# Loading the first B tile already cast, halving the B loads and reordering the right half in the head of a matmul + RMSNorm kernel on Trainium2

## The chip, the cores and the metric

The kernel runs on one core of one Trainium2 chip. The metric is the device time of one execution in microseconds (us). "Run time" below is that metric; "span" is the length of the traced part of an execution, about 1.8 us shorter. All positions ("at 39.46") are microseconds from the start of the span.

## The reference, cut to what matters

```python
m, k, n = 2048, 2048, 2048          # a, b, gamma are float32, eps = 1e-5
def reference(a, b, gamma, eps):
    x = np.matmul(a, b)
    rms = np.sqrt(np.mean(x ** 2, axis=-1, keepdims=True) + eps)
    return (gamma * x / rms).astype(np.float32)
```

## The kernel before

Sixteen blocks of 128 rows of A are multiplied by B. Most of the work (the later rows) uses seven products of quarter matrices instead of eight. The change touches only the **head**: the first four row blocks (rows 0 to 511), which are computed while B streams in for the first time.

- B comes in 16 tiles of 256 rows by 1024 columns: eight for the left half of its columns, eight for the right half. GpSimd issues these loads, which cast float32 to bf16 on the way (software-queue loads). Tile 0 of the left half is the exception: it is loaded as float32 on a hardware queue and cast by two engines.
- The **left half** has eight contraction steps. Step k needs the transposed A tile k and B tile k; within step k, PE also transposes A tile k+1. A step is 16 matmuls and 8 transposes.
- The **right half** has eight steps of 8 plain matmuls (row blocks 0 and 1) and three product matmuls (P2, P5 and P1 of row blocks 2 and 3; P1 lags one step).
- The **exit**: after the eighth right step come products 4, 3, 7 and 6. Meanwhile ScalarE and VectorE empty the banks, compute row norms of the next A block and scale it to 16 bits. PE transposes that block in the middle of product 7. I call this place the **turn**.

```python
# a0f: fp32 landing place of A tile 0; b0f: the same for B tile 0
nc.sync.dma_start(out=a0f, in_=a[0:HB * P, 0:W2].rearrange("(r p) k -> p r k", p=P))
for t in range(2):
    nc.scalar.dma_start(out=b0f[t], in_=b[t * P:(t + 1) * P, 0:HALF])

def load_b(j, kp):                       # one load for a whole B tile
    nc.gpsimd.dma_start(
        out=raw[j][kp],
        in_=b[kp * W2:(kp + 1) * W2, j * HALF:(j + 1) * HALF].rearrange("(t p) n -> p t n", p=P))

def load_head(kp):                       # A tile, then B tile
    nc.gpsimd.dma_start(out=ah(kp), in_=a[0:HB * P, kp * W2:(kp + 1) * W2].rearrange(...))
    load_b(0, kp)
# ... (cut: identities, 11 warm-up matmuls)

def transpose_first():
    # ... (cut: 8 fp32 transposes of A tile 0 into two banks)
    for t in range(2):
        cast_first = [lambda: nc.vector.tensor_copy(out=raw[0][0][:, t, :CH], in_=b0f[t][:, :CH]),
                      lambda: nc.scalar.copy(out=raw[0][0][:, t, CH:], in_=b0f[t][:, CH:])]
        move = [...]                     # (cut) VectorE moves the transposed A tile
        for work in (cast_first + move if t == 0 else move + cast_first):
            work()

# left half, per step kp (cut): load two to four tiles ahead, transpose_head(kp + 1) in its middle,
# 14 matmuls into 7 banks and 2 into a part bank

def stream_right(kp):
    order = [(g, kt) for kt in (2 * kp, 2 * kp + 1) for g in plain]
    if kp in (0, KP - 1):
        order.sort(key=lambda x: plain.index(x[0]))
    if kp == KP - 1:
        for m in (2, 5):
            pair_matmul(m, kp)
        pair_matmul(1, kp - 1)
    for g, kt in order:
        # ... plain matmul
    if kp < KP - 1:
        for m in (2, 5):
            pair_matmul(m, kp)
        if kp > 0:
            pair_matmul(1, kp - 1)
    else:
        pair_matmul(1, kp)

# exit
nc.scalar.copy(out=x22, in_=pair[2])
nc.vector.tensor_tensor(out=x22, in0=pair[5], in1=x22, op=ALU.add)
evict(plain, (2, 3))                     # banks 0, 1 by ScalarE; 2, 3 by VectorE
b_sums_in_place(1, KP - 1)
product(PAIR, 1, 4, pair[2], start=False)
row_norm(HB); row_norm(HB + 1)           # ScalarE
nc.vector.tensor_tensor(out=x22, in0=pair[1], in1=x22, op=ALU.subtract)
row_factor(HB)
product(PAIR, 1, 3, pair[5], start=False)
row_apply(HB)                            # VectorE: the 128x2048 scaling to fp16
# ... (cut)
product(PAIR, 1, 7, p7, within={5: [lambda: turn(HB, 0)]})
turn(HB, 1)
# ... (cut: product 6 and the whole body)
```

Of the kernel before, what the change touches and what calls it, by code (L numbers as in the profile page):

```python
# [17 lines left out]
def kernel(  # L18
# [13 lines left out]
    nc = tc.nc  # L32
# [32 lines left out]
    sums = [t_left, t_right]  # L65

    a0f = early[:, 0:2048].bitcast(FP32).rearrange("p (r k) -> p r k", r=HB)
    b0f = [early[:, 2048 + t * 2048:2048 + (t + 1) * 2048].bitcast(FP32) for t in range(2)]
    NAH = 6
    ah_slot = [early[:, 6144 + s * 1024:6144 + (s + 1) * 1024].rearrange("p (r k) -> p r k", r=HB)  # L70
               for s in range(NAH)]
# [16 lines left out]
        return (at_even, at_odd)[(mb // 2) % 2][:, mb % 2]  # L88


    nc.sync.dma_start(out=a0f, in_=a[0:HB * P, 0:W2].rearrange("(r p) k -> p r k", p=P))
    for t in range(2):
        nc.scalar.dma_start(out=b0f[t], in_=b[t * P:(t + 1) * P, 0:HALF])

    def ah(kp):
        return ah_slot[(kp - 1) % NAH]

    def load_b(j, kp):
        nc.gpsimd.dma_start(  # L99
            out=raw[j][kp],  # L100
            in_=b[kp * W2:(kp + 1) * W2, j * HALF:(j + 1) * HALF].rearrange(
                "(t p) n -> p t n", p=P))

    def load_head(kp):
        nc.gpsimd.dma_start(  # L105
            out=ah(kp),
            in_=a[0:HB * P, kp * W2:(kp + 1) * W2].rearrange("(r p) k -> p r k", p=P))
        load_b(0, kp)
# [16 lines left out]

        nc.gpsimd.tensor_copy(out=pace, in_=src)

    load_head(1)
    identity_f = t_left[:, 2, KP - 1, 0:2 * P].bitcast(FP32)
    make_identity(nc, identity_f)  # L130
    for kp in range(2, 4):
        load_head(kp)
    warm = sq_pool.tile([P, 2 * CH], BF16, name="sq")
# [7 lines left out]


    warm_bank = ps_a.tile([P, CH], FP32, name="acc")
    for _ in range(11):
        nc.tensor.matmul(warm_bank, warm[:, 0:P], warm[:, 0:CH], start=True, stop=True)

    gamma_sb = consts.tile([P, N], FP32, name="gamma_sb")
# [2 lines left out]
    def transpose_first():  # L150
        bank = [ps_t.tile([P, CH], FP32, name="tbank"), ps_a.tile([P, CH], FP32, name="acc")]
        view = [b.rearrange("p (r m) -> p r m", r=HB) for b in bank]
        for t in range(2):
            for r in range(HB):
                nc.tensor.matmul(view[t][:, r, :], a0f[:, r, t * P:(t + 1) * P], identity_f,
                                 is_transpose=True, start=(r == 0), stop=(r == HB - 1))
        for t in range(2):
            cast_first = [lambda: nc.vector.tensor_copy(out=raw[0][0][:, t, :CH],
                                                        in_=b0f[t][:, :CH]),
                          lambda: nc.scalar.copy(out=raw[0][0][:, t, CH:], in_=b0f[t][:, CH:])]  # L160
            move = [lambda h=h: nc.vector.tensor_copy(
                out=head_at[:, t, 2 * h:2 * h + 2, :], in_=view[t][:, 2 * h:2 * h + 2, :])
                for h in range(2)]
            for work in (cast_first + move if t == 0 else move + cast_first):
                work()

    def transpose_head(kp):
        bank = ps_t.tile([P, CH], FP32, name="tbank")
# [218 lines left out]
    def new_bank():  # L387
        return ps_a.tile([P, CH], FP32, name="acc")
# [74 lines left out]

    def stream_right(kp):

        order = [(g, kt) for kt in (2 * kp, 2 * kp + 1) for g in plain]
        if kp in (0, KP - 1):
            order.sort(key=lambda x: plain.index(x[0]))
        if kp == KP - 1:
            for m in (2, 5):  # L470
                pair_matmul(m, kp)
            pair_matmul(1, kp - 1)
        for g, kt in order:
            if kt == 0:
                banks[g] = new_bank()
            head_matmul(banks[g], *g, kt)
        if kp < KP - 1:
            for m in (2, 5):
                pair_matmul(m, kp)
            if kp > 0:  # L480
                pair_matmul(1, kp - 1)
        else:
            pair_matmul(1, kp)

    for kp in range(KP):
        load_later(1)
# [344 lines left out]
```

## Time and profile before

| | before |
|---|---|
| median run time | 222.89 us of three runs (222.73 to 223.05); with three more beside the changed kernel 222.63 us (222.40 to 223.05) |
| traced execution | run 222.97 us, span 221.2 us |
| first head matmul | 7.54 us |
| second left step starts | 12.30 us |
| sixth left step starts | 28.99 us |
| right half starts | 40.25 us |
| product 4 starts | 59.27 us |
| turn (transposes of the next A block) | 63.84 us |

The page's busy table, kernel before (engine, busy us, share of the span, instructions). PE is the bound.

```profile
PE 210.0 (95%) x1035; PEld 97.7 (44%) x1035; DVE 167.4 (76%) x330; ACT 128.1 (58%) x263; POOL 29.4 (13%) x59
```

The timeline of PE, kernel before. Each line is a group of like instructions: start, busy us, line, operation, output and inputs, count, and in brackets the idle time before it with what ended it.

```profile
7.54 2.88 PE L384 MATMUL acc<-b,head_at 128*128 128x512 bf16 x12
...
12.30 1.67 PE L384 MATMUL acc<-b,head_at 128*128 128x512 bf16 x7
...
16.19 1.67 PE L384 MATMUL acc<-b,head_at 128*128 128x512 bf16 x7
...
25.10 1.67 PE L384 MATMUL acc<-b,head_at 128*128 128x512 bf16 x7 [0.85 <-DMA b<-in_b_dram]
...
28.99 1.67 PE L384 MATMUL acc<-b,head_at 128*128 128x512 bf16 x7
...
40.25 1.89 PE L384 MATMUL acc<-b,head_at 128*128 128x512 bf16 x8
...
59.27 3.62 PE L289 MATMUL acc<-early,head_at 128*128 128x512 bf16 x16
...
63.84 0.62 PE L189 MATMUL tbank<-identity_h,head_at 128*128 128x128 f16 x8
```

A left step takes PE 3.90 us when nothing makes it wait (16.19 minus 12.30, 28.99 minus 25.10). The one long wait, 0.85 us, is for a B tile. The waits view of the weight loads (total us, times, longest):

```profile
PEld L189 <- DVE head_at L244: 0.4, 1, 0.4
```

The timeline of GpSimd, kernel before. It has eight loads in flight and holds the next one until an old one lands, so the ends of its idle times show when loads land.

```profile
12.54 0.70 POOL L99 DMA_DIRECT2D b<-in_b_dram  x1 [1.77 <-DMA b<-in_b_dram]
...
16.37 0.70 POOL L99 DMA_DIRECT2D b<-in_b_dram  x1 [1.78 <-DMA b<-in_b_dram]
```

A pair of A and B tiles lands every 3.83 us here (the next pairs take 4.06 and 4.91 us, then 3.82 again).

The windows view, kernel before. After the stretch and a granted clock come busy shares of PE, PEld, DVE, ACT and POOL with instruction counts, then PEclk, the mean busy share of the DMA engines, and GB/s moved.

```profile
5.00:6.00 1.00, 0.87 (x4) 0.10 (x2) 0.74 (x1) 0.62 (x1) 1.00 (x2) 1.00 1.12 337
6.00:7.00 1.00, 0.60 (x6) 0.63 (x7) 0.00 (x0) 0.00 (x0) 1.00 (x10) 1.00 0.78 196
```

At the start the queues still move float32 and reach 337 GB/s; once all loads cast, they settle near 200 GB/s written, twice that read.

### The profile page before, as it was taken

Reading aid. Unit: us, or ns where it says so; the run is one execution under the profiler, and the core shown is the slowest. Engines: PE = TensorE matmul, PEld = TensorE weight load, DVE = VectorE, ACT = ScalarE, POOL = GpSimd, SP = SyncE. Lnnn points to the kernel's source line nnn. Section 1 sums busy time; section 2 is a strip of 40 time slices with the busy share of each in tenths; the row PEclk is TensorE's granted clock in tenths of the full one; section 3 lists DMA queues with packets and bytes.
Section 4 is the critical chain, followed back from the end, with each engine's and each line's share of the span. In section 5 each row is a group of like instructions: output and inputs, shape, how many; then the busy total and the mean of one; then the engine's idle time right before and its main releaser. Section 6 shows DMA issues by size and latency. Waiting matters only on the chain.

```text
span 221.2 us, 3022 instructions
## 1 busy us (share of the span) xinstructions
PE 210.0 (95%) x1035; PEld 97.7 (44%) x1035; DVE 167.4 (76%) x330; ACT 128.1 (58%) x263; POOL 29.4 (13%) x59
## 2 busy tenths in 40 slices
PE   7899899999999999999999999999999999999950
PEld 2445454444455444444444444444444444444430
DVE  2428789999988898969696639855794759797691
ACT  3110001830698898678945997389738995334570
POOL 7634323220000001200110002000200000000040
PEclk9999999999999999999999999999999999999996
DMA  6999999999938596956799249955798349044045
GB/s 184 223 202 209 203 208 210 211 211 238 426 114 357 187 291 120 316 230 150 219 308 397 79 88 266 367 221 95 187 302 367 69 90 381 32 190 193 1 190 191
DMA packets 36321, 47.13 MB, mean 213 GB/s; under 512 B 21969, under 2 KB 26065, under 8 KB 34897
## 3 DMA queue, kind: packets, MB, share of 16 engines
q0 software_dynamic: 9936, 23.33, 41.7%
q1 hardware_dynamic: 25936, 22.29, 33.6%
q10 hardware_dynamic: 432, 1.31, 2.0%
q8 instruction: 8, 0.13, 0.2%
q14 instruction: 9, 0.07, 0.1%
HBM read 34.60 MB, written 16.78 MB: 232 GB/s over the span
## 4 chain that ended last, share of the span: by engine, by line
PE 83%; DMA 8%; POOL 3%; DVE 2%; issue 1%; ACT 1%; DVEq 0%; ACTq 0%; POOLq 0%
PE acc L289 69%; PE acc L384 12%; DMA b<-in_b_dram 8%; POOL early L105 1%; POOL b L99 1%; DVE x L709 1%; PE tbank L415 1%; PE tbank L172 1%; DVE x L712 1%; ACT sq L307 0%; PE tbank L189 0%; PE acc L189 0%; DVE a L709 0%; ACT sq L778 0%; DVE x L786 0%
## 5 line engine op out<-in xcount | busy, mean ns | idle before, releaser
L289 PE MATMUL acc<-b,s 128*128 128x512 bf16 x408 | 92.1, 379 | 0.0
L289 PEld LDWEIGHTS <-s 128*128 128x128 f16 (+1 forms) x512 | 49.9, 98 | 59.9 <-DVE s L264 0.4
L384 PE MATMUL acc<-b,head_at 128*128 128x512 bf16 x176 | 41.9, 379 | 1.0 <-DMA b<-in_b_dram 0.9
L307 ACT ACTIVATE sq<-x 128x512 bf16<-128x512 f32 x54 | 34.0, 630 | 6.9 <-DVE x L709 3.0
L366 DVE SCALAR_TENSOR_TENSOR x<-x,r,gamma_sb 128x1024 f32<-128x1024 f32 x28 | 34.8, 1281 | 0.7
L223 ACT ACTIVATE sq<-a 128x1024 bf16<-128x1024 f32 x24 | 25.3, 1054 | 2.4 <-DMA a<-in_a_dram 1.9
L384 PEld LDWEIGHTS <-head_at 128*128 128x128 bf16 x176 | 16.8, 98 | 20.6 <-issue 1.9
L246 ACT ACTIVATE head_at<-a,s 128x2048 f16<-128x2048 f32 x10 | 20.0, 1998 | 3.7 <-DVE s L233 3.7
L426 ACT COPY x<-acc 128x512 f32<-128x512 f32 x6 | 3.4, 586 | 25.7 <-PE acc L384 25.7
L289 PEld LDWEIGHTS <-head_at 128*128 128x128 f16 (+1 forms) x112 | 10.9, 98 | 13.2
L289 PE MATMUL acc<-early,head_at 128*128 128x512 bf16 x64 | 14.5, 379 | 0.0
L289 PEld LDWEIGHTS <-at_even 128*128 128x128 f16 x96 | 9.4, 98 | 11.3
L289 PE MATMUL acc<-early,s 128*128 128x512 bf16 x56 | 14.4, 379 | 0.0
L264 DVE TENSOR_TENSOR s<-head_at 128x1024 f16<-128x1024 f16 (+5 forms) x22 | 13.4, 635 | 0.1
L596 DVE TENSOR_TENSOR x<-x,x 128x512 f32<-128x512 f32 x9 | 6.2, 692 | 8.8 <-ACT x L594 8.3
L99 POOL DMA_DIRECT2D b<-in_b_dram x15 | 10.6, 706 | 16.0 <-DMA b<-in_b_dram 13.4
L578 ACT COPY x<-acc 128x512 f32<-128x512 f32 x9 | 5.2, 574 | 11.6 <-PE acc L289 11.5
L289 PE MATMUL acc<-t_left,s 128*128 128x512 bf16 x48 | 11.3, 379 | 0.0
L280 DVE TENSOR_TENSOR b<-b 128x1024 bf16<-128x1024 bf16 x16 | 10.8, 684 | 0.2
L289 PE MATMUL acc<-t_left,head_at 128*128 128x512 bf16 x48 | 10.9, 379 | 0.0
L289 PE MATMUL acc<-t_left,at_even 128*128 128x512 bf16 x48 | 10.8, 379 | 0.0
L289 PE MATMUL acc<-early,at_even 128*128 128x512 bf16 x48 | 10.8, 379 | 0.0
(111 smaller groups left out, 216.7 us busy)
## 6 DMA issues: line engine op xcount, KB each, us to landing
out_dram<-x SPq DMA_DIRECT2D x30, 512.0 KB, 3.8
a<-in_a_dram POOLq DMA_DIRECT2D x10, 1024.0 KB, 8.7
b<-in_b_dram POOLq DMA_DIRECT2D x15, 512.0 KB, 17.5
a<-in_a_dram POOLq DMA_DIRECT2D x4, 512.0 KB, 16.6
early<-in_a_dram POOLq DMA_DIRECT2D x7, 256.0 KB, 14.8
early<-in_b_dram ACTq DMA_DIRECT2D x2, 512.0 KB, 5.9
gamma_sb<-in_gamma_dram POOLq DMA_DIRECT2D x1, 1024.0 KB, 14.8
early<-in_a_dram SPq DMA_DIRECT2D x1, 512.0 KB, 5.5
```

The source lines that it names most:

```text
L99: nc.gpsimd.dma_start(out=raw[j][kp], in_=b[kp * W2:(kp + 1) * W2, j * HALF:(j + 1) * HALF].rearrange("(t p) n -> p t n", p=P))
L223: nc.scalar.activation(out=junk, in_=a32[mb][:, h * HALF:(h + 1) * HALF], func=ACTF.Square, scale=2.0 ** -8, accum_out=n2[:, h:h + 1])
L246: nc.scalar.activation(out=a16[mb], in_=a32.pop(mb), func=ACTF.Copy, scale=factor.pop(mb))
L264: nc.vector.tensor_tensor(out=sum_of(g, s)[:, lo:hi, :], in0=x[:, lo:hi, :], in1=y[:, lo:hi, :], op=op)
L280: nc.vector.tensor_tensor(out=flat[:, 1:3, :], in0=flat[:, 1:3, :], in1=flat[:, 0::3, :], op=ALU.add)
L289: nc.tensor.matmul(bank, lhsT[:, kp, :], rhs, start=(start and kp == 0), stop=(kp == KP - 1), skip_group_check=not start)
L307: nc.scalar.activation(out=sq[:, 0:CH], in_=src, func=ACTF.Square, scale=inv_sqrt_n, accum_out=msq[mb][:, c:c + 1])
L366: nc.vector.scalar_tensor_tensor(out=x, in0=x, scalar=inverse_of[mb], in1=gamma_sb[:, h * HALF:(h + 1) * HALF], op0=ALU.mult, op1=ALU.mult)
L384: nc.tensor.matmul(bank, head_at[:, kt, r, :], head_rhs(c, kt), start=(kt == 0), stop=(kt == KT - 1))
L426: copy(out=x_chunk(*g), in_=banks[g])
L578: nc.scalar.copy(out=c, in_=one[1])
L596: nc.vector.tensor_tensor(out=t, in0=t, in1=x12, op=ALU.add)
```

## The change

The intent: start the head sooner and let PE begin on half a B tile. B tile 0 comes by the same casting loads as the others, so its landing place and four casts go. A tile 0 comes by halves on the two hardware queues. Every B tile comes in two half loads of 128 rows. In the right half each step uses the first half tile, then P2 (which needs only that half), then the second half, then P5. Warm-up matmuls go from eleven to eight.

```diff
-    nc.sync.dma_start(out=a0f, in_=a[0:HB * P, 0:W2].rearrange("(r p) k -> p r k", p=P))
-    for t in range(2):
-        nc.scalar.dma_start(out=b0f[t], in_=b[t * P:(t + 1) * P, 0:HALF])
+    for h, queue in enumerate((nc.sync, nc.scalar)):
+        queue.dma_start(out=a0f[:, 2 * h:2 * h + 2, :],
+                        in_=a[2 * h * P:(2 * h + 2) * P, 0:W2].rearrange("(r p) k -> p r k", p=P))
 
     def load_b(j, kp):
-        nc.gpsimd.dma_start(
-            out=raw[j][kp],
-            in_=b[kp * W2:(kp + 1) * W2, j * HALF:(j + 1) * HALF].rearrange(
-                "(t p) n -> p t n", p=P))
+        for t in range(2):
+            lo = kp * W2 + t * P
+            nc.gpsimd.dma_start(out=raw[j][kp][:, t, :],
+                                in_=b[lo:lo + P, j * HALF:(j + 1) * HALF])
 
-    load_head(1)
+    load_b(0, 0)
     identity_f = t_left[:, 2, KP - 1, 0:2 * P].bitcast(FP32)
     make_identity(nc, identity_f)
+    load_head(1)
 
-    for _ in range(11):
+    for _ in range(8):
         nc.tensor.matmul(warm_bank, warm[:, 0:P], warm[:, 0:CH], start=True, stop=True)
 
     # (cut) in transpose_first the four casts go; VectorE and ScalarE each move one transposed bank
 
     def stream_right(kp):
-        # (cut) the order of before, shown above
+        def plain_matmuls(order):
+            for g, kt in order:
+                if kt == 0:
+                    banks[g] = new_bank()
+                head_matmul(banks[g], *g, kt)
+
+        first, second = ([(g, 2 * kp + t) for g in plain] for t in range(2))
+        if kp == 0:
+            plain_matmuls(x for both in zip(first, second) for x in both)
+            pair_matmul(2, kp)
+            pair_matmul(5, kp)
+            return
         if kp == KP - 1:
             pair_matmul(1, kp - 1)
+        plain_matmuls(first)
+        pair_matmul(2, kp)
+        plain_matmuls(second)
+        pair_matmul(5, kp)
+        pair_matmul(1, kp if kp == KP - 1 else kp - 1)
```

More of the change, by code (lines that the diff above doesn't have):

```diff
@@ L67 @@
     a0f = early[:, 0:2048].bitcast(FP32).rearrange("p (r k) -> p r k", r=HB)
-    b0f = [early[:, 2048 + t * 2048:2048 + (t + 1) * 2048].bitcast(FP32) for t in range(2)]
     NAH = 6
@@ L156, in transpose_first @@
                                  is_transpose=True, start=(r == 0), stop=(r == HB - 1))
-        for t in range(2):
-            cast_first = [lambda: nc.vector.tensor_copy(out=raw[0][0][:, t, :CH],
-                                                        in_=b0f[t][:, :CH]),
-                          lambda: nc.scalar.copy(out=raw[0][0][:, t, CH:], in_=b0f[t][:, CH:])]
-            move = [lambda h=h: nc.vector.tensor_copy(
-                out=head_at[:, t, 2 * h:2 * h + 2, :], in_=view[t][:, 2 * h:2 * h + 2, :])
-                for h in range(2)]
-            for work in (cast_first + move if t == 0 else move + cast_first):
-                work()
+        for t, copy in enumerate((nc.vector.tensor_copy, nc.scalar.copy)):
+            for h in range(2):
+                copy(out=head_at[:, t, 2 * h:2 * h + 2, :], in_=view[t][:, 2 * h:2 * h + 2, :])
     def transpose_head(kp):
@@ L464, in stream_right @@
     def stream_right(kp):
-        order = [(g, kt) for kt in (2 * kp, 2 * kp + 1) for g in plain]
-        if kp in (0, KP - 1):
-            order.sort(key=lambda x: plain.index(x[0]))
+        def plain_matmuls(order):
[9 more added lines that the diff above has]
+            return
         if kp == KP - 1:
-            for m in (2, 5):
-                pair_matmul(m, kp)
             pair_matmul(1, kp - 1)
-        for g, kt in order:
-            if kt == 0:
-                banks[g] = new_bank()
-            head_matmul(banks[g], *g, kt)
-        if kp < KP - 1:
-            for m in (2, 5):
-                pair_matmul(m, kp)
-            if kp > 0:
-                pair_matmul(1, kp - 1)
-        else:
-            pair_matmul(1, kp)
+        plain_matmuls(first)
[3 more added lines that the diff above has]
+        pair_matmul(1, kp if kp == KP - 1 else kp - 1)
     for kp in range(KP):
```

## The prediction

> **What bounds the kernel now.** PE. The busy table gives it 210.0 of 221.2 us; the chain of waits is PE alone from 25.10 to 208.16 us. What can move is the head, 0 to 59 us. The timeline shows PE starting a left contraction step at 12.30, 16.19, 20.18, 25.10, 28.99, 32.89 us: 3.90 us each (16 matmuls and 8 transposes), but for one of 4.9 us, in which PE waited 0.85 us for B. GpSimd's idle periods end as B tiles land: 12.54, 16.37, 20.43, 25.34, 29.16 us, so 3.82 us a step. The windows view shows about 207 GB/s written there, all casting. In the right half PE takes 2.37 us a step and DMA 2.48. Before 12.30 PE idles 1.46 us at the start, 0.53 for A0, and about 1 us more.
>
> **What the change does.**
> 1. B0 arrives cast: four casts go (0.62+0.74, 0.62+0.43 us on ACT and DVE); the second pair began only at 8.70 us, when the fp32 B0 landed. A0's transposed tiles are moved by DVE and ACT. The source bytes stay. I estimate DMA work until B1 has landed from the rates seen (about 420 GB/s for fp32, 207 written for casts): 7.6 us before, 7.6 after. So no bandwidth is won; order is.
> 2. A0 no longer competes with fp32 B0 on the other hardware queue. All queues share the DMA engines, as the Trainium skill says (DMA: Bandwidth & Descriptors, "Issuing engines are not separate DMA queues"); here A0 landed at 6.4 us, after B0's first half at 5.2. I expect A0 near 5.0, first head matmul near 6.3 (was 7.54), B1's step near 10.8 (was 12.30).
> 3. Half loads: PE may start a step one half (about 1.25 us) before the whole tile has landed. The second half is needed about 1.9 us into the step. That slack swallows the 0.85 us wait.
> 4. The right half needs the last tile's second half for only 6 matmuls (1.3 us), before for nearly 12.
> 5. Eight warm-ups end near 4.9 us. The trace shows the faster weight loads from 5.27. The Trainium skill (TensorE: Matmul & The Clock Gate, Part 1) puts the release after about 3.4 us of activity, so eight barely suffice.
>
> **How much survives.** PE could be 2.3 us early at the fifth step. Then: the first right step takes both halves of its tile at once (cost about 0.4 us); DVE has no idle time from 37.0 to 61.7 us and PE already waits 0.4 us on the scaled A rows at 63.8 us, so another 0.4 us may go there. The rest, PE-bound, moves along. Net estimate: 1.5 us.
>
> **Prediction: 221.4 us, 220.4 to 222.7 (8 in 10). Faster by over 2%: 0.01; within 2%: 0.97; slower: 0.02.**
>
> **What would show it.** Right: first head matmul before 6.6 us, second contraction step before 11.2 us, no wait over 0.5 us on B at the fifth step, product 4 starting near 57.6 us (was 59.27). Wrong: B0's first half landing after 7 us (step 2), B waits in each step (3), long PE waits near 60 us (survival), matmuls 0.43 us apart after 6 us (5).
>
> **What would make it wrong.** Sixteen more software DMAs lower the rate; GpSimd has only eight loads in flight (it held its ninth until the first landed), now 4 MB of source, before 6; the software B0 starts late; a cold PE costs up to 1.5 us. Upward: the 4.9 us step was chance.

## The result, and the profile after

| | before | after |
|---|---|---|
| median run time, six runs each | 222.63 us (222.40 to 223.05) | 222.84 us (222.60 to 222.93) |
| ratio after / before | | 1.0006 (95%: 0.9993 to 1.0019) |
| traced execution: run, span | 222.97, 221.2 us | 222.79, 221.0 us |

Ratios here and below are the mean time of one kernel's fast runs over that of the other's in the same rounds, so they are not quite the ratio of the medians quoted beside them. The time did not move.

The busy table of the page, kernel after: the same PE time, slightly less VectorE and ScalarE work (the casts are gone), more GpSimd (the additional loads).

```profile
PE 210.2 (95%) x1032; PEld 98.1 (44%) x1032; DVE 165.5 (75%) x326; ACT 127.2 (58%) x263; POOL 35.7 (16%) x76
```

The timeline of PE, kernel after, at the same places.

```profile
6.55 3.20 PE L378 MATMUL acc<-b,head_at 128*128 128x512 bf16 x12
...
11.68 1.67 PE L378 MATMUL acc<-b,head_at 128*128 128x512 bf16 x7
13.69 0.62 PE L166 MATMUL tbank<-identity,early 128*128 128x128 bf16 x8 [0.34 <-DMA early<-in_a_dram]
...
23.89 1.67 PE L378 MATMUL acc<-b,head_at 128*128 128x512 bf16 x7
...
28.20 1.67 PE L378 MATMUL acc<-b,head_at 128*128 128x512 bf16 x7
...
39.46 1.89 PE L378 MATMUL acc<-b,head_at 128*128 128x512 bf16 x8
...
58.45 3.62 PE L283 MATMUL acc<-early,head_at 128*128 128x512 bf16 x16
...
63.55 0.62 PE L183 MATMUL tbank<-identity_h,head_at 128*128 128x128 f16 x8 [0.40 <-DVE head_at L238]
```

Against this one trace of before, PE is 0.99 us ahead at its first head matmul, 0.62 at the second left step, 0.79 at the sixth, 0.79 at the right half and 0.82 at product 4. At the turn the lead is 0.29 us, because a 0.40 us wait has appeared. Two things are to be explained: why a start about a microsecond sooner and the removal of a 0.85 us wait do not add up in the left half, and why half a microsecond is lost between 58 and 64 us.

The waits view of the weight loads: first the line for the A tiles in the kernel before, then in the kernel after (total us, times, longest).

```profile
PEld L172 <- DMA early<-in_a_dram: 0.2, 1, 0.2
```

```profile
PEld L166 <- DMA early<-in_a_dram: 3.1, 7, 0.8
```

In the kernel after, the weight loads of the transposes wait for their A tile in all seven left steps. The wait for B became a wait for A. PE itself loses time at two of them: 0.50 us in the second step (at 13.69) and 0.40 us in the fifth (at 25.80; the view puts that wait down to VectorE's L269, which ended 0.04 us after the A tile had landed; in e1, e3 and e5 it names the A tile). Together that is the 0.92 us, within rounding, by which the sixth step is later than four steps of 3.90 us after the second.

The windows view, kernel after, same stretches as before.

```profile
5.00:6.00 1.00, 1.00 (x7) 1.00 (x6) 0.06 (x1) 0.00 (x0) 1.00 (x2) 1.00 1.00 92
6.00:7.00 1.00, 1.00 (x6) 0.63 (x5) 0.70 (x2) 0.20 (x1) 1.00 (x3) 1.00 0.84 84
```

For two microseconds the casting loads move 92 and 84 GB/s, less than half of the 203 GB/s that the same view shows between 8 and 9 us. The busy share of the DMA engines is 1.00 and 0.84 there, 1.39 between 8 and 9 us.

The chain of waits between 57 and 69 us, first before, then after (start, us, what).

```profile
57.49 1.73 PE acc L384 x8
59.22 4.75 PE acc L289 x22
63.97 0.49 PE tbank L189 x8
```

```profile
58.18 0.23 PE acc L283
...
58.50 0.69 DVE x L507
...
59.71 0.68 DVE x L420
60.39 0.60 DVE b L274
60.99 0.60 DVE x L513
...
62.21 1.29 DVE head_at L238
...
63.55 0.62 PE tbank L183 x8
```

Before, the chain stays on PE. After, it leaves PE at the exit and goes through VectorE's bank work and scaling until the turn.

What heads that chain shows in the timelines of ScalarE and VectorE. The first fence is of before, the second of after. The first line of each is ScalarE's copy of P2's bank, the second VectorE's addition of P5 to it.

```profile
57.10 0.59 ACT L511 COPY x<-acc 128x512 f32<-128x512 f32 x1 [10.60 <-PE acc L289]
...
58.68 0.68 DVE L512 TENSOR_TENSOR x<-acc,x 128x512 f32<-128x512 f32 x1
```

```profile
57.35 0.59 ACT L506 COPY x<-acc 128x512 f32<-128x512 f32 x1 [11.64 <-PE acc L283]
...
58.50 0.69 DVE L507 TENSOR_TENSOR x<-acc,x 128x512 f32<-128x512 f32 x1 [0.47 <-ACT x L420]
```

PE is 0.82 us ahead, yet the copy starts 0.25 us *later*. In the old eighth step P2 and P5 were finished before the plain matmuls; now P2 ends after half of them and P5 after all. VectorE is only 0.18 us ahead.

### The profile page after: what moved, and what is told of

Read it like the earlier page. It is cut to its first block, busy times and chain, and to the rows that moved or that the text cites. A ratio compares the mean times of both kernels' runs of the same rounds, so it can differ in the third digit from the quotient of the medians.

```text
span 221.0 us, 3043 instructions
## 1 busy us (share of the span) xinstructions
PE 210.2 (95%) x1032; PEld 98.1 (44%) x1032; DVE 165.5 (75%) x326; ACT 127.2 (58%) x263; POOL 35.7 (16%) x76
## 4 chain that ended last, share of the span: by engine, by line
PE 80%; DMA 9%; DVE 5%; POOL 2%; issue 1%; ACT 1%; DVEq 0%; ACTq 0%; POOLq 0%
PE acc L283 67%; PE acc L378 11%; DMA early<-in_a_dram 4%; DMA b<-in_b_dram 4%; POOL b L100 1%; DVE x L704 1%; PE tbank L409 1%; PE tbank L166 1%; POOL early L104 1%; DVE head_at L238 1%; DVE x L707 1%; DVE t_left L269 0%; PE tbank L183 0%; ACT sq L301 0%; PE acc L183 0%
## 5 line engine op out<-in xcount | busy, mean ns | idle before, releaser
L283 PE MATMUL acc<-b,s 128*128 128x512 bf16 x408 | 93.2, 379 | 0.0
L378 PE MATMUL acc<-b,head_at 128*128 128x512 bf16 x176 | 43.3, 381 | 0.0
L100 POOL DMA_DIRECT2D b<-in_b_dram x32 | 17.2, 539 | 20.3 <-DMA b<-in_b_dram 14.4
L283 PEld LDWEIGHTS <-head_at 128*128 128x128 f16 (+1 forms) x112 | 10.9, 98 | 13.2
L125 POOL COPY pace<-x 128x1 f32<-128x1 f32 x4 | 1.7, 413 | 66.3 <-DVE x L600 65.1
L274 DVE TENSOR_TENSOR b<-b 128x1024 bf16<-128x1024 bf16 x16 | 10.8, 683 | 0.2
L283 PE MATMUL acc<-t_left,head_at 128*128 128x512 bf16 x48 | 10.9, 379 | 0.0
L283 PE MATMUL acc<-t_left,at_even 128*128 128x512 bf16 x48 | 10.8, 379 | 0.0
```

The costliest lines, as they stand in the source:

```text
L100: nc.gpsimd.dma_start(out=raw[j][kp][:, t, :], in_=b[lo:lo + P, j * HALF:(j + 1) * HALF])
L274: nc.vector.tensor_tensor(out=flat[:, 1:3, :], in0=flat[:, 1:3, :], in1=flat[:, 0::3, :], op=ALU.add)
L283: nc.tensor.matmul(bank, lhsT[:, kp, :], rhs, start=(start and kp == 0), stop=(kp == KP - 1), skip_group_check=not start)
L378: nc.tensor.matmul(bank, head_at[:, kt, r, :], head_rhs(c, kt), start=(kt == 0), stop=(kt == KT - 1))
```

## The experiments

"Before" in each table is the kernel before, run on the same chip. No difference below reaches 1%, so the milestones of the traces, one trace per kernel, carry most of the argument. Two theories of the left half stood against each other.

- **Supply.** The left half ends when its bytes have come. A and B are the same bytes in both kernels, so a lead at the start is spent on waiting for tiles.
- **Head.** The lead is only smaller than it should be, because the first software loads are slow; a faster start would carry through.

For the exit: **order** (the new eighth step delays the banks) against **chance** or a cost of the earlier arrival itself.

### e8_before_again: is the trace of before typical?

No edit.

> The kernel before, unchanged, for a second trace: its profiled run was 0.3 us above the median of its later runs. If the 0.85 us wait for B at the fifth step (25.1 us) is its regular behaviour, it is here again with 0.5 to 1.1 us; if it was chance, it is below 0.3 us and the kernel before reaches product 4 at about 58.4 us instead of 59.27, with nothing left to gain from slack there.

| | before | e8 |
|---|---|---|
| median | 222.49 us (222.29 to 223.00) | 222.45 us (222.34, 222.57) |
| ratio | | 0.9997 (0.998 to 1.0014) |

The wait for B at the fifth step was there again (0.6 us), so it is regular in being there, not in its length. And the first trace was of a late run: this one starts its sixth left step at 28.58 (28.99 there), product 4 at 58.83 (59.27 there) and the turn at 63.40 (63.84 there). Most of that lateness lies in the long step itself: 0.08 us at the second step, 0.16 at the fourth, 0.41 at the fifth, and no more than 0.44 from there on. Against it the changed kernel leads by 0.38 us at product 4 and is 0.15 us *behind* at the turn. That, and not the 0.29 us against the first trace, agrees with the medians.

### e1_right_old: the right half in its old order

```diff
 def stream_right(kp):          # body of the kernel before; half loads and the new head stay
-        first, second = (...)
+        order = [(g, kt) for kt in (2 * kp, 2 * kp + 1) for g in plain]   # ... as before
```

> The change without its right-half order: matmuls of the right half as before, half loads and the new head kept. Exit theory (the change loses its lead at the end of the right half, because products 2 and 5 and the four plain banks now finish later relative to product 4, so ScalarE and VectorE start the copies, the row norms and the scaled A rows later): product 4 starts near 58.5 us as in the changed kernel, perhaps up to 0.3 later because the last tile's second half is needed at once, but VectorE no longer idles 0.47 us at 58 us, PE waits under 0.15 us on the scaled A rows (0.40 in the changed kernel), and the time is 0.3 to 0.6 us below the changed kernel, 0.3 to 0.8 below the kernel before. Rival (the row norms are late for a reason outside the right half's order, by DMA or ScalarE): the PE wait stays near 0.4 us and the time stays within 0.15 us of the changed kernel.

| | before | e1 |
|---|---|---|
| median | 222.56 us (222.36 to 223.02) | 223.05 us (222.28 to 224.15) |
| ratio | | 1.0025 (1.0002 to 1.0049) |

The wait at the turn is gone (turn at 63.42). But the time became longer and scattered by nearly 2 us. The trace, that of the 224.15 us run, shows new PE waits of 0.73 us at 77.23 and 0.46 us at 83.05. The source is a load that GpSimd issues near 64 us, told under e3.

### e3_exit_old: only the eighth right step in its old order

```diff
         if kp == KP - 1:
+            for m in (2, 5):
+                pair_matmul(m, kp)
             pair_matmul(1, kp - 1)
+            plain_matmuls(x for both in zip(first, second) for x in both)
+            pair_matmul(1, kp)
+            return
         plain_matmuls(first)
         pair_matmul(2, kp)
         plain_matmuls(second)
         pair_matmul(5, kp)
-        pair_matmul(1, kp if kp == KP - 1 else kp - 1)
+        pair_matmul(1, kp - 1)
```

> The change with only the last step of the right half (the eighth) in its order of before: products 2 and 5 first, then product 1 of the step before, then the plain products bank by bank. Exit theory: as in the run with the whole old right order, the PE wait on the scaled A rows goes under 0.15 us, and the time is 0.3 to 0.5 us below the changed kernel, against at most 0.3 us of new PE waiting for the last tile's second half. Rival: PE waits near 0.4 us all the same and the time is within 0.15 us of the changed kernel.

| | before | e3 |
|---|---|---|
| median | 222.56 us | 223.77 us (222.82 to 224.85) |
| ratio | | 1.0053 (1.0031 to 1.0075) |

Again the turn's wait went (turn at 63.28) and again the time rose. Two lines of this trace, of GpSimd and of VectorE, then the line of GpSimd in the kernel after:

```profile
64.14 1.57 POOL L119 DMA_DIRECT2D a<-in_a_dram  x1 [10.78 <-ACT x L522]
...
64.31 1.28 DVE L238 TENSOR_SCALAR head_at<-a,s 128x2048 f16<-128x2048 f32 x1
```

```profile
64.40 0.53 POOL L119 DMA_DIRECT2D a<-in_a_dram  x1 [11.32 <-DVE s L226]
```

Issuing the load took 1.57 us where it takes 0.53 elsewhere, and it ended 0.12 us after VectorE's 128x2048 scaling (64.31 + 1.28 = 65.59; 64.14 + 1.57 = 65.71). The Trainium skill, page "SBUF — State Buffer", sections "SBUF: two separate sides" and "A bandwidth-pool intuition that's wrong (but worth ruling out)", warns of this as the "DVE blocks DMA" trap: a load issued by GpSimd needs descriptors, GpSimd cannot write them while VectorE holds the port that they share, and the wait lasts until "DVE-end + ~115 ns". This trace agrees within its rounding. In the traces without the trouble in which GpSimd issues this load, it began at least 0.25 us ahead of VectorE (e10; 0.35 us or more in all others), here and in e1 only 0.17 us. The A block came late: ScalarE began its norms at 71.62 us, in the kernel after at 70.13, in e1 at 71.90. PE then waited 0.60 us at 76.95 and 0.46 us at 82.77.

### e5_sync_loads: that block by a hardware queue

On top of e3 (`load_block` is given the queue as an argument; cut):

```diff
-    load_block(HB + 2)
-    load_block(HB + 3)
+    load_block(HB + 2, nc.sync)
+    load_block(HB + 3, nc.sync)
```

> The run with the eighth right step in its old order lost its PE wait at 63 us but ended 1 us later, with 1.57 us (0.53 in the changed kernel) for GpSimd's issue of the next A block and a PE wait of 0.6 us near 77 us. Here the same kernel issues that block and the one after it from the SyncE hardware queue. Port theory (GpSimd's descriptor writing is locked out by VectorE's 1.28 us scaling of an A block, which starts 0.17 us after the issue, so the block lands about 1.5 us late): the PE waits near 77 and 82.5 us go, the row norms of that block start before 70.5 us (71.6 there), the time falls to about 222.0 us, 0.2 to 0.5% under the kernel before, and the scatter (222.8 to 224.9 there) shrinks to under 0.6 us. Rival (the block is late because the queue or HBM is slow at that time): ScalarE still starts on the block after 71.2 us and the time stays above 223.

| | before | e5 |
|---|---|---|
| median | 222.49 us (222.29 to 223.00) | 222.55 us (222.38 to 222.96) |
| ratio | | 1.0003 (0.9991 to 1.0015) |

The waits near 77 and 83 us are gone and the scatter is down from 2.0 to 0.6 us. The lock is thus the reason for e3's longer time, and for e1's, where the same issue took 1.57 us, too. The hoped-for gain over before did not come: product 4 starts at 58.77 us. In this trace the right half began late, at 39.76 us, and took 19.01 us, as in the kernel before (19.02). In e1 and e3 it began at 39.60 and 39.38 us but took 19.25 and 19.33; the likely reason is that the old order needs the last half tile of B at once (e3's waits show 0.17 us for it, e1's none). All three reach product 4 between 58.71 and 58.85 us, hardly sooner than e8 (58.83).

### e7_old_head: the old head, the rest of the change

The kernel before with half loads and the new right order; A tile 0, B tile 0 and the warm-ups as before.

```diff
 def load_b(j, kp):
-        nc.gpsimd.dma_start(out=raw[j][kp], in_=...)
+        for t in range(2):
+            lo = kp * W2 + t * P
+            nc.gpsimd.dma_start(out=raw[j][kp][:, t, :], in_=b[lo:lo + P, j * HALF:(j + 1) * HALF])
 def stream_right(kp):
-    ...    # order of before
+    ...    # order of after
```

> Half loads and the new right-half order with the head of before (B0 in fp32 on the ScalarE queue, A0 in one piece, 11 warm-ups). If the new head gives the lead of about 0.6 us at the second step that the two traces show, this kernel starts the second step at 12.0 to 12.4 us; its A tiles then land just in time, the right half starts about 0.2 to 0.6 us later than in the changed kernel, and it is 0.1 to 0.5 us slower than it. If the head's lead is lost to the A tiles anyway, both reach the right half within 0.15 us of each other, and the times agree within 0.15 us.

| | before | e7 |
|---|---|---|
| median | 222.49 us (222.29 to 223.00) | 223.01 us (222.91 to 223.13) |
| ratio | | 1.0022 (1.0009 to 1.0035) |

This is the cleanest evidence of the exit's cost. First fence: e7. Second: the kernel before of e8.

```profile
58.82 3.62 PE L289 MATMUL acc<-early,head_at 128*128 128x512 bf16 x16
...
63.92 0.62 PE L189 MATMUL tbank<-identity_h,head_at 128*128 128x128 f16 x8 [0.40 <-DVE head_at L244]
```

```profile
58.83 3.62 PE L289 MATMUL acc<-early,head_at 128*128 128x512 bf16 x16
...
63.40 0.62 PE L189 MATMUL tbank<-identity_h,head_at 128*128 128x128 f16 x8
```

Product 4 starts at the same time, the turn 0.52 us later, and the medians differ by 0.52 to 0.56 us. The order costs this without any lead, so it is no cost of arriving early. Nor is it the half loads, in which e7 also differs from e8: e1, e3 and e5 have them with the old order and no wait at the turn. The half loads gained nothing with the old head: the sixth left step starts at 28.57, and at 28.58 in e8. Against the kernel after, e7 differs in the head alone. The kernel after is 0.60 us ahead of it at the second step and 0.37 us at the sixth, at the right half and at product 4 (58.45 against 58.82), as the first branch of the expectation had it. By time it is 0.17 us ahead, by medians. So part of the head's lead does come through.

### e2_turn_late: give the turn the time that it lacks

```diff
-    product(PAIR, 1, 7, p7, within={5: [lambda: turn(HB, 0)]})
+    product(PAIR, 1, 7, p7)
+    turn(HB, 0)
     turn(HB, 1)
```

> The change with the first transposes of the scaled A rows after product 7 instead of inside it (0.65 us later). If the 0.40 us PE wait on these rows is what ate the lead, PE has no wait there over 0.15 us and the time falls by 0.2 to 0.45 us below the changed kernel, unless the later transposes create a new wait of PE in front of the next group's first product, which the wait view would show at VectorE's sums near 68 to 71 us. If the lead had been lost for another reason, no change within 0.1 us.

| | before | e2 |
|---|---|---|
| median | 222.56 us | 222.18 us (221.97 to 222.36) |
| ratio | | 0.9982 (0.997 to 0.9994) |

PE does product 7's last three matmuls first and the scaled rows are there when it comes to them:

```profile
58.37 3.62 PE L283 MATMUL acc<-early,head_at 128*128 128x512 bf16 x16
61.83 1.89 PE L283 MATMUL acc<-b,s 128*128 128x512 bf16 x8
63.55 0.61 PE L183 MATMUL tbank<-identity_h,head_at 128*128 128x128 f16 x8
```

There is no wait, and 0.38 us are won against before, by medians, which is the size of the changed kernel's lead at product 4 against e8 (58.83 to 58.45). So that lead is real, and the exit order had spent it. (The later turn was not tried in the kernel before, whose PE has no wait there to save.) Interesting besides: this head is the same as in the kernel after, but its PE clock was released sooner. PE was ready for its first head matmuls 0.8 us before they started, waited 0.81 and 0.57 us for the two halves of B tile 0, and its second left step came at 12.01, later than 11.68. The cold clock was not the limit: in the kernel after, the weight loads for A tile 1 waited 0.58 us until 9.84, so a faster PE would have met a tile that was not there.

### e10_p5_early: is it P5 alone?

```diff
         pair_matmul(2, kp)
+        if kp == KP - 1:
+            pair_matmul(5, kp)
         plain_matmuls(second)
-        pair_matmul(5, kp)
+        if kp < KP - 1:
+            pair_matmul(5, kp)
```

> The change, but in the eighth right step product 5 goes ahead of the four plain matmuls of the second half, so that VectorE need not wait for it at 58 us. If product 5 behind is alone the cause of the 0.40 us wait at the exit, the wait falls under 0.1 us and the time by 0.3 us or more. If ScalarE's chain (copy of product 2, two banks, row norms, ready at 61.47 in the changed kernel) is just as late, because the plain banks end together at the end of the step, the wait stays between 0.25 and 0.6 us and the time within 0.15 us of the changed kernel.

| | before | e10 |
|---|---|---|
| median | 222.59 us (222.24 to 222.77) | 222.76 us (222.44 to 223.63) |
| ratio | | 1.0014 (0.9999 to 1.0028) |

The turn's wait stays at 0.5 us (turn at 63.60). P5 late is not shown to be the cause alone. The test of it is not clean: in this trace VectorE also waited 0.66 us for B's last half tile at 56.96 and was late for that reason. But ScalarE's line is as late: its copy of P2 and of two plain banks precede the norms, which are ready at 61.47 us in the kernel after and at 61.41 in e10, against 61.14 in e8. Only the old order of the whole step (e1, e3) or a later turn (e2) takes the wait away.

### e4_a_early: the A tile ahead of the second half of B

```diff
     # (cut) load_b takes the halves to load as a third argument
     def load_head(kp):
         # A tile kp first, as before
-        load_b(0, kp)
+        if kp > 1:
+            load_b(0, kp - 1, (1,))
+        load_b(0, kp, (0,))
+        if kp == KP - 1:
+            load_b(0, kp, (1,))
```

> The change with one swap in the left half's load order: each A tile goes ahead of the second half of the B tile before it. Theory (in the left half PE is now held by the A tile, which lands behind both halves of the previous B tile and is needed 1.5 us into the step, so the half loads cannot give their slack): the PE waits on A at about 13.7 and 25.8 us go, the right half starts 0.3 to 0.5 us earlier than in the changed kernel (39.46), product 4 too, and the time falls by 0.2 to 0.5 us, since the exit chain hangs on PE and moves along. Rival (DMA supply as a whole is the limit, whatever the order): the start of the right half moves by less than 0.15 us.

| | before | e4 |
|---|---|---|
| median | 222.56 us | 222.40 us (222.08 to 222.80) |
| ratio | | 0.9988 (0.9975 to 1.0001) |

PE's waits for A in the left steps are gone. In its trace, however, B tile 0's first half landed only at 8.03 us (5.82 to 7.30 in the other kernels with this head). PE waited 1.89 us for it and the second step began at 12.53 us, the latest of all kernels. Nevertheless its sixth step began at 28.14 us and its right half at 39.49, like the others: they had lost their lead by then. But this trace ran from the second step on at 3.90 us a step without a wait, so here the start set the sixth step, not the supply. Whether this load order would let a lead through, e9 and e12 can tell, which have it too. The next table has all traces with the whole A tiles.

| trace | second step | plus 4 x 3.90 us | sixth step, measured | lost in between |
|---|---|---|---|---|
| before | 12.30 | 27.90 | 28.99 | 1.09 |
| e8 (before again) | 12.22 | 27.82 | 28.58 | 0.76 |
| e7 | 12.28 | 27.88 | 28.57 | 0.69 |
| after | 11.68 | 27.28 | 28.20 | 0.92 |
| e1 | 11.62 | 27.22 | 28.35 | 1.13 |
| e3 | 11.49 | 27.09 | 28.13 | 1.04 |
| e5 | 11.59 | 27.19 | 28.51 | 1.32 |
| e2 | 12.01 | 27.61 | 28.13 | 0.52 |
| e6 | 12.26 | 27.86 | 28.38 | 0.52 |
| e10 | 11.79 | 27.39 | 28.14 | 0.75 |
| e11 | 10.88 | 26.48 | 28.18 | 1.70 |
| e4 (A tile ahead) | 12.53 | 28.13 | 28.14 | 0.01 |
| e9 (A tile ahead) | 11.69 | 27.29 | 27.71 | 0.42 |
| e12 (A tile ahead) | 11.82 | 27.42 | 27.51 | 0.09 |

With the new head and the load order of the change (after to e11 in the table), the second step's start varies by 1.38 us, the sixth's by 0.38, and it does not follow it: PE takes up what lands. With the A tile ahead, 0.01 to 0.42 us are lost instead of 0.52 to 1.70, and two of three traces reach the sixth step 0.4 to 0.6 us sooner than any without it, with the same bytes. So it is not the bytes alone, "whatever the order", that hold PE. A reason fits: in both orders the third load of a step lands about 2.6 us after the first (18.74 to 21.34 in the kernel after). As an A tile it is needed 1.5 us into the step, as the second half of B 1.95 us into it. The swap is worth the difference, an estimate of 0.45 us. From there PE keeps its own pace: 11.26 us to the right half both before and after.

### e6_pool_pause: do descriptors make the first loads slow?

GpSimd issues the loads of tiles 2 and 3 only after the first transposed A tile has been stored:

```diff
     load_head(1)
-    for kp in range(2, 4):
-        load_head(kp)
     ...
     transpose_first()
+    wait_for(head_at[:, 0, 0, 0:1])
+    for kp in range(2, 4):
+        load_head(kp)
```

> The change, but GpSimd issues the loads after the second contraction tile only once the first transposed A tile has been stored (about 6.3 us), so that it writes no descriptors from about 5 to 6.3 us. In the changed kernel the software queue moves only about 45 KB per half microsecond from 4.5 to 7 us, against 100 before and after. Theory A (GpSimd's descriptor writing slows the queue's transfers at that time): the rate from 5 to 6.5 us goes above 80 KB per half microsecond, A1 lands about 1 us earlier, the second contraction step starts before 11 us (11.68 in the changed kernel). Theory B (something else, such as memory being slow then for these rows): the slow stretch stays at 4.5 to 7 us, and the second step starts within 0.4 us of 11.68. The time moves by at most 0.4 us either way, because the wait for A tiles and the exit of the right half take most of a lead.

| | before | e6 |
|---|---|---|
| median | 222.49 us | 223.15 us (222.59 to 224.13) |
| ratio | | 1.0035 (1.0016 to 1.0053) |

The slow stretch stayed: 107 and 117 GB/s in the two windows, inside the spread of the nine other traces with this head, these rows of B and whole A tiles (76 to 119 and 84 to 122), when GpSimd was busy for 0.20 and 0.36 of them instead of all. Writing later descriptors is not what makes it slow. The second step began at 12.26 us.

### e11_b0_other_rows: the first loads from other rows (wrong result)

B tile 0 is read from B's last 256 rows, so the result is wrong; the work is otherwise the same.

```diff
-            lo = kp * W2 + t * P
+            lo = (kp if (j, kp) != (0, 0) else KP - 1) * W2 + t * P
```

> A wrong result on purpose: the changed kernel with the first B tile read from the last 256 rows of B instead of the first. In the changed kernel the software queue moves this tile at about half the later rate from 4.5 to 7 us, with single packets of over 2 us near 4.9 us. If those rows of B are what is slow, the slow stretch and the long packets go. If it is the time or the start of the queue, they stay, and the second contraction step starts at 11.4 to 12.6 us as before.

One run of 222.74 us (state unknown, one run), before 222.59 us. The two windows moved 117 and 167 GB/s instead of 92 and 84; the second is outside the spread of the other traces. No packet took over 2 us, as two do in the kernel after, but e3 and e10 have no such packet either and are slow all the same. The head got what the prediction had wanted:

```profile
10.88 1.67 PE L378 MATMUL acc<-b,head_at 128*128 128x512 bf16 x7
13.78 0.62 PE L166 MATMUL tbank<-identity,early 128*128 128x128 bf16 x8 [1.22 <-DMA early<-in_a_dram]
```

The second step starts 0.80 us sooner than in the kernel after, and at once PE waits 1.22 us for the A tile instead of 0.34. The right half starts at 39.44 us (39.46 in after), product 4 at 58.43 (58.45). In this trace the head's lead was worth nothing. That is not yet a refutation of the head theory, because the slow stretch had only moved. The windows view of e11:

```profile
10.00:12.00 2.00, 1.65 (x9) 0.71 (x8) 0.40 (x1) 0.58 (x1) 0.87 (x5) 1.00 1.09 124
```

The kernel after has 204 GB/s in this stretch. So A tile 2 landed at 13.73 us, no sooner than in the kernel after (13.64), and PE, which was early, waited for it. Why some loads are slow at the start, and whether B's first rows have to do with it, stays open: this is one run.

### e13_half_a_after and e14_half_a_before: fewer bytes (wrong results on purpose)

If supply is the limit, fewer bytes must let a lead through. Both kernels load only half of each left A tile and fill the rest with a constant. By source bytes a step's supply falls by one sixth, from 3.83 us to an estimate of 3.2 us. e13 is the kernel after so changed, e14 the kernel before.

```diff
-            out=ah(kp),
-            in_=a[0:HB * P, kp * W2:(kp + 1) * W2].rearrange("(r p) k -> p r k", p=P))
+            out=ah(kp)[:, 0:2, :],
+            in_=a[0:2 * P, kp * W2:(kp + 1) * W2].rearrange("(r p) k -> p r k", p=P))
     ...    # (cut) at the start, on VectorE:
+    for slot in ah_slot:
+        nc.vector.memset(slot[:, 2:4, :], 0.5)
```

> A wrong result on purpose: the changed kernel with only the first two of the four row blocks of each A tile of the left half loaded (the rest is set to a constant on VectorE at the start), so a left step needs 1.25 MiB of source instead of 1.5 and supply is about 3.2 us a step by the rate seen, against 3.90 of PE. Supply theory: no PE wait for A or B after the second step, steps of 3.90 us, the right half starts at 27 us after the second step, so at 38.0 to 38.8 us (39.46 in the changed kernel), and product 4 at most 57.8 us (58.45). Rival (PE or VectorE hold the steps): the right half still starts after 39.2 us.

> The same in the kernel before (wrong result on purpose). Supply theory: its second step starts at about 12.0 us and the right half 27 us later, at 38.8 to 39.4 us (39.84 and 40.25 in its two traces), so that with supply out of the way the changed kernel reaches the right half earlier by the whole lead of its second step, 0.4 to 1.0 us. Rival: it starts the right half after 39.7 us, or both kernels start it within 0.2 us of each other.

| | before | e13 (after, half A) | e14 (before, half A) |
|---|---|---|---|
| median | 222.84 us (222.34 to 223.18) | 221.91 us (221.28 to 222.11) | 221.55 us (221.47 to 221.69) |
| ratio to before | | 0.9954 (0.993 to 0.9978) | 0.9942 (0.9918 to 0.9965) |

Timelines of PE, e13 first, e14 second:

```profile
57.03 3.62 PE L285 MATMUL acc<-early,head_at 128*128 128x512 bf16 x16
...
62.12 0.62 PE L185 MATMUL tbank<-identity_h,head_at 128*128 128x128 f16 x8 [0.40 <-DVE head_at L240]
```

```profile
58.01 3.62 PE L291 MATMUL acc<-early,head_at 128*128 128x512 bf16 x16
...
62.58 0.62 PE L191 MATMUL tbank<-identity_h,head_at 128*128 128x128 f16 x8
```

Neither trace has a wait for A or B in the left steps. The second steps start at 11.07 and 12.16 us, the sixth at 26.78 and 27.76, the right halves at 38.03 and 39.02: the lead is now carried through, and 0.98 us of it arrive at product 4. With fewer bytes a lead comes through, as supply expects; so it does with the A tile ahead (e12, table under e4), and here, too, the A tile comes sooner. Then the exit's order takes its 0.5 us as before, and 0.46 us are left at the turn. This rests on two traces. In time the lead is not shown: e13's traced run took 221.28 us, 0.41 us less than e14's 221.69, as the traces have it, but its three other runs took 221.89 to 222.11, longer than all four of e14. They have no trace, and why stays open.

### e9_turn_late_a_early: both mends

e2 and e4 together.

> The change with both repairs: each A tile ahead of the second half of the B tile before it, and the first transposes of the scaled A rows after product 7. If the two losses are separate (A tiles hold PE in the left half; the scaled A rows hold it at the exit), PE has neither wait, the steps run at 3.90 us from the second on except for what the start costs, and the time is 221.6 to 222.2 us, at or below the run with the late transposes alone (222.18) and 0.15 to 0.4% below the kernel before. If the DMA supply fixes the start of the right half whatever the order, it equals the run with the late transposes alone within 0.15 us.

| | before | e9 |
|---|---|---|
| median | 222.59 us (222.24 to 222.77) | 221.95 us (221.59 to 222.71) |
| ratio | | 0.9976 (0.9963 to 0.999) |

This version beats the kernel before by about a quarter of a per cent (and the kernel after, whose ratio to before was 1.0006). The right half starts at 39.19 us and product 4 at 58.19; no wait for A is left among PE's, and none at the turn. The sixth left step:

```profile
27.71 1.67 PE L382 MATMUL acc<-b,head_at 128*128 128x512 bf16 x7
```

That is 0.42 us sooner than in e2 (28.13), whose loads have the order of the change. In time the gain of the A tile ahead is not shown apart: e9's ratio to before, 0.9976, and e2's, 0.9982, have intervals that overlap.

### e12_all_sync: e9 with the two blocks on a hardware queue

```diff
-    load_block(HB + 2)
-    load_block(HB + 3)
+    load_block(HB + 2, nc.sync)
+    load_block(HB + 3, nc.sync)
```

> The kernel with both repairs, and the next two A blocks issued from the SyncE hardware queue. Against the kernel with both repairs alone: if no issue of GpSimd meets VectorE's scaling there, both have the same time within 0.15 us and the same scatter; if some of its runs do meet it, this one is faster on the median and its scatter is smaller.

| | before | e12 |
|---|---|---|
| median | 222.59 us | 221.85 us (221.54 to 223.67) |
| ratio | | 0.9986 (0.9958 to 1.0013) |

In time this is inconclusive. The trace has the earliest milestones of all kernels with whole A tiles: sixth step 27.51 us, right half 39.00, product 4 57.99. Five of six runs took 221.54 to 222.38 us and one took 223.67. The scatter is not smaller than e9's, so where the lock does not bite, the other queue buys nothing that these runs could show.

## Why the prediction was right or wrong

Predicted were 221.4 us (220.4 to 222.7), measured 222.84: of the 1.5 us that were to be won, nothing came.

**Right: what bounds the kernel, the first head matmul, and that the change stays within 2%.** The first head matmul came at 6.55 us (predicted near 6.3, test: before 6.6). It was not safe: in e10, with the same head, it came at 7.35, held by B tile 0. A tile 0 was there at 4.85 us at the latest (predicted near 5.0): its first transpose began then, straight after the warm-ups and without a wait. The prediction rested here on the Trainium skill, "DMA: Bandwidth & Descriptors", section "Issuing engines are not separate DMA queues", and this trace agrees: A tile 0, freed of the float32 loads of B beside it, came at least 1.5 us sooner (before, PE waited for it until 6.40 us). How much of that is due to its being split over two queues, no run shows.

**Wrong, and it decides the case: "PE could be 2.3 us early at the fifth step."** The fifth step began 1.21 us early (23.89 against 25.10), and one step later 0.79 us was left; against the second trace of before it was 0.80 and 0.38 us. The sum was 1.5 us for B1's step plus 0.85 us for the swallowed wait. Both terms were too large.

- *Term one, B1's step near 10.8 us:* measured 11.68, a lead of 0.62 instead of 1.5 us. The first software loads moved at less than half their later rate for two microseconds. e11 did reach 10.88 us, but its later loads came no sooner and it did not help.
- *Term two, the slack of half loads:* the wait at the fifth step did go, but the lead that it should have left was spent on waits for A. Tile k+1 of A lands behind both halves of B tile k and is needed 1.5 us into step k. The prediction looked at the needs of B alone.
- *Adding them:* this was the error in reasoning. The prediction itself said "no bandwidth is won; order is", with 3.82 us of supply and 3.90 of work per step. When supply and work run at one pace, a lead lasts only until PE meets a load that has not landed, and that was the A tile. The table under e4 shows it: with the load order of the change the sixth step begins at 28.1 to 28.5 us after a second step anywhere from 10.9 to 12.3. With the A tile ahead (e9, e12) it begins at 27.7 and 27.5, and with fewer bytes (e13 against e14) the full 0.98 us came through. Each of these rests on one trace per kernel.

**Wrong in the other direction: "the first right step takes both halves of its tile at once (cost about 0.4 us)".** The lead is 0.79 us at the start of the right half and 0.82 at product 4. Nothing was lost there.

**Right in size, wrong in reason: "another 0.4 us may go there", at the scaled A rows.** Against the first trace 0.53 us went (0.82 to 0.29), and e7 against e8 shows 0.52 us with no lead at all. The prediction took it for VectorE's lack of idle time, and for the growth of a wait that PE "already" had at 63.8 us; that 0.4 us was a wait of the weight loads, and PE had none. It is the order of the eighth right step: it finishes P2, P5 and all plain banks late, while the norms and the scaling queue behind them on two engines.

**The sum, done again.** Predicted: 2.3 - 0.4 - 0.4 = 1.5 us. Measured against the first trace: 0.79 - 0.53 + 0.03 (right half) = 0.29 us. And that trace was 0.4 us later than its repeat; against the repeat it is 0.38 - 0.53 = -0.15 us, and the medians have +0.21 us of time. The prediction took one traced run for the kernel: "Upward: the 4.9 us step was chance" named the danger: the step was longer in both traces of before, but 0.25 of its 0.85 us of waiting were chance (0.60 in the second trace).

**Wrong but harmless: eight warm-ups "barely suffice".** The Trainium skill ("TensorE: Matmul & The Clock Gate", Part 1) says that the release comes after about 3.4 us of activity and varies from run to run. Here the weight loads of the kernel after stay slow until about 7.3 us, so that two of its head matmuls after 6 us were 0.43 and 0.34 us apart instead of 0.22, the prediction's own sign against it. In e2, with the same head, PE is fast at 4.75. The slow one started its second step sooner (11.68 against 12.01), because both waited for loads.

**The wait at the fifth step itself.** In the traces of before, e8 and after, the DMA records hold one packet of the queue that fetches instructions just ahead of it. The DMA view of before, for 20 to 26 us, lists it (packets, MB, share of 16 engines' time in the window):

```profile
q8 instruction: 1, 0.02, 1.0%
```

1.0% of 16 engines over 6 us is about 0.96 us on one engine (0.975 in the record, at 21.47 us; in e8 0.936 us at 21.22). If a tile has landed only when the slowest of the engines has, one engine's 0.96 us can shift all later landings. In the kernel after the packet came at 23.04 us, and the pause between two B landings is longer just there: step five to step six took 4.31 us instead of 3.90. The timing fits in these three, but the packet alone is not enough. All 16 traces have it, between 20.80 and 23.58 us. In eleven the next landings come 0.6 to 1.3 us late; in five (e2, e4, e6, e10, e11) they come on time, and PE's next step takes its 3.90 us in four of these (3.93 in e11). No experiment moved the packet, so this cause is argued, not shown.

## What to carry to other kernels

Before counting a lead, ask whether the stage that it enters is paced by work or by supply: if the two paces are within a few per cent (3.83 and 3.90 us here), an earlier start and a removed wait can be the same microsecond. Write down for every load, not only for the one that is being changed, when it lands and when it is needed. Here one swap in the order of the loads let most of a lead through in the traces, and so did fewer bytes. When an order is changed so that inputs are consumed as they come, look at what it finishes last: banks that are done late hold up the engines behind PE, and 0.5 us were lost there. And compare milestones against two traces of the old kernel, since one run can be 0.4 us late from a single wait on.

## What the Trainium skill lacked or had wrong

- **"Runtime: NRT & Kernel Launch", section "Instruction fetch mechanics".** It calls the cost of crossing a 16 KiB instruction block "mostly hidden". It does not say that the fetch goes through one of the engines that carry the data loads. Here one such packet held an engine for 0.94 to 0.98 us, and a wait of 0.85 us (0.6 in the repeat) on a full load queue followed it in each trace of the kernel before. The link is by timing only: in five of the 16 traces no landing is late after the packet, and the trace does not name the engine that carried it.
- **"SBUF — State Buffer", the "DVE blocks DMA" trap.** It is right, and its 115 ns agree with the 0.12 us here. Its example of a trigger is a float32 copy; here it was a float32 to fp16 scaling by a per-row scalar (128x2048, 1.28 us), and the issue took 1.57 instead of 0.53 us. It does not say how much sooner GpSimd has to begin: 0.17 us ahead of VectorE was not enough, 0.25 us was (e10).
- **"DMA: Bandwidth & Descriptors".** I found nothing there on why casting loads at the start of a program run at half their later rate: 92 and 84 GB/s between 5 and 7 us, 203 later. Reading other rows of B gave 117 and 167 in one run, and 124 between 10 and 12 us, where the kernel after has 204. The cause is open.
- **"TensorE: Matmul & The Clock Gate", Part 1.** It says that the release varies by run, and it does: before 4.75 us in one run and near 7.3 us in another with the same eight warm-ups. That is wider than the ±500 ns which the page gives for the transition point; its remark in the same Part that one kernel showed 6, 11 or 14 slow matmuls fits better.
